# A list scheduler for TensorE's order in a hybrid sequence-mixing layer

## The chip, the cores and the metric

One core of a Trainium2 chip runs the whole layer. The metric is the device time of one execution in microseconds; lower is better. 1493.49 us is the median of three runs of the kernel before.

## What is computed

The input is x, 1024 frames of 1024 channels in float32; 16 learned frames are put in front (L = 1040). Each frame is RMS-normalised, and one projection (`w_in`, 1024 x 7832) gives the inputs of three groups of heads, which run side by side on it. Their outputs, 2048 channels together, go through one output projection (`w_out`), are RMS-normalised and added to the input.

```
hn = rms_norm(h, norm_pre[l])
proj = jnp.einsum("bld,dp->blp", hn, w_in[l])
p_a, p_b, p_c = jnp.split(proj, _splits([P_A, P_B, P_C]), axis=-1)
mixed = jnp.concatenate([
    gated_deltanet_group(p_a, dn_conv[l], dn_A_log[l], dn_dt_bias[l], dn_norm[l]),
    rwkv7_group(p_b, rw_mu[l], rw_w0[l], rw_w2[l], rw_a0[l], rw_a2[l],
                rw_k_k[l], rw_k_a[l], rw_r_k[l], rw_ln_w[l], rw_ln_b[l]),
    mamba2_group(p_c, mb_conv[l], mb_conv_b[l], mb_dt_bias[l], mb_A_log[l], mb_D[l], mb_norm[l]),
], axis=-1)
out = jnp.einsum("blm,md->bld", mixed, w_out[l])
h = h + rms_norm(out, norm_post[l])
```

Group a has 6 heads of 128, group b 8 of 64, group c 12 of 64. Group a is a gated delta rule: in every chunk of frames a triangular system is solved, and a 128 x 128 state is carried from chunk to chunk. Group b is a recurrence with a state per head, done in chunks of 64 frames with a triangular solve as well. Group c is a chunked state-space scan without a solve.

## The kernel before, in words

**Units.** The work after the setup is cut into twelve units: a0 to a5 (one head of group a each), b0 to b3 (two heads of group b), c0 and c1 (six heads of group c), and a thirteenth, o, the output projection. Each unit is a Python generator (`unit_a`, `unit_b`, `unit_c`, `unit_o`) that issues instructions and yields where it would have to wait.

**Projections.** The projection is cut into 61 tiles of 128 output channels. `proj` (line 156) does a tile in pieces of frames, three each (FULL or REAL, 340 to 348 frames, and others for group b), in a PSUM bank `pj`. Float32 accuracy comes from three products in the fast float32r format for each of 8 slices of the inner dimension: rounded weights by rounded input (`hh`), rounded weights by the input's residue (`hl`), the weights' residue by `hh`; 24 products a piece, 72 a tile, in the order slice by slice. `weights` (line 142) loads a tile's weights in two halves: a load on SP, two copies on ScalarE (ACT), and an accumulating load on POOL's queue that leaves the residue. After a tile's first piece, `prefetch` asks for the next tile's weights. Behind each piece an evacuation (`conv`, `shifted` or a gate) takes it out of PSUM on ACT and VectorE (DVE).

**Scans.** A unit first needs some tiles ("proj"), then runs its scan with small float32 products, which TensorE does in two passes each: products of 32x32 and 64x64 that finish the triangular solve (`am`, `bm`), products of 64x128 (`bgr`), transposes (`akT`, `cxT`, ...), and a recurrence over the chunks in which a product, an evacuation on ACT or DVE and the next product follow each other (`aks`, `av`, `ads` in a; `bsi`, `bu`, `bd` in b; `cds`, `cof`, `cdg` in c). `solve32` does the inner 32 x 32 triangular solves on DVE, two small instructions (`s_tmp`, `alb` or `blb`) for each of 30 columns, after a round trip of the blocks through DRAM on SP. In the middle of its scan a unit asks for more tiles with `later` (values, queries, gates), with a due time, and waits for them with `wait`.

**What orders the work.** `schedule` (line 1171) steps the generators by an estimated clock: `Meter` adds up what TensorE's instructions take and a rough lag of the others, and a scan whose lag is over goes ahead of the projection ("fill"), one product of which is issued at a time. `safe` admits a unit only if the 26 tiles of the `s` pool suffice for it. Up to two lanes with two PSUM banks each serve the scans; a third scanning unit shares a lane. So the kernel gives each instruction a place in the program and a priority (`PRI`, `EVA`, `CALM`); which instruction an engine really takes next is then chosen by the framework, which simulates the program with its own estimates and takes, on each engine, the ready instruction with the best priority. That holds for all engines, TensorE's included.

**End.** `unit_o` (line 1080) computes the first half of the output's columns from the mixes that are finished (`po<-ow,ome`), holds until all scans have ended, then does the second half with all sixteen mixes and the rest of the first (`po<-ow,omw`), and writes the output.

## Time and profile before

| | |
|---|---|
| median of 3 runs | 1493.49 us (1492.66 to 1499.25) |
| profiled execution | 1497.37 us, span 1495.2 us |
| TensorE (PE), matmuls | 1439.9 us in flight, 96% of the span, 9657 instructions |
| VectorE (DVE) | 954.8 us, 64% |
| ScalarE (ACT) | 707.2 us, 47% |
| mean granted TensorE clock | 0.956 |
| projection products (pj) | 4392 |
| output products (po) | 768 |

How to read it: the span runs from the first to the last instruction of the profiled execution; the time is a little longer by what lies around it. A matmul in flight is not a matmul at its peak: they are pipelined, and what one costs in a stream is the distance from its start to the next start. PEld is the load of the weights into the array, which runs beside matmuls. The clock is the share of full speed that the chip granted.

### The profile page before, as it was taken

How to read it: one execution, taken by the hardware profiler on the slowest of the kernel's cores; microseconds unless marked ns; L12 is line 12 of the kernel's file. 1: busy time of each engine (PE TensorE's matmuls, PEld its weight loads, DVE VectorE, ACT ScalarE, POOL GpSimd, SP SyncE). 2: the span in 40 equal slices, each digit the busy share in tenths (PEclk: the TensorE clock that was granted, in tenths of full speed). 3: DMA queues.
4: the chain of work that ended last, by engine and by line, in shares of the span. 5: the costliest groups of instructions: out<-in, count | busy, mean ns of one | idle time of the engine just before them, and what ended most of it. 6: DMA issues, size and time to landing. Idle time of an engine off the chain costs nothing.

```text
span 1495.2 us, 26098 instructions
## 1 busy us (share of the span) xinstructions
PE 1439.9 (96%) x9657; PEld 1274.6 (85%) x9657; DVE 954.8 (64%) x2688; ACT 707.2 (47%) x1936; POOL 173.4 (12%) x227
## 2 busy tenths in 40 slices
PE   5999999999999999999999999999999999999897
PEld 4999888888888789989888899889999988678686
DVE  6549485376768347869735787546588867542573
ACT  6455361345444364344746543544577255532530
POOL 2111000000001011111101111001132100200100
PEclk9999898799999799999979999889999999899999
DMA  7344332123223222434322244114534322553851
GB/s 225 87 114 85 81 61 58 43 62 93 51 46 75 67 71 72 116 65 103 76 86 57 62 85 96 29 43 99 118 97 105 71 58 59 171 162 89 259 191 57
DMA packets 120449, 136.28 MB, mean 91 GB/s; under 512 B 39867, under 2 KB 72379, under 8 KB 120323
## 3 DMA queue, kind: packets, MB, share of 16 engines
q1 hardware_dynamic: 102755, 102.64, 23.2%
q0 software_dynamic: 17568, 31.99, 12.7%
q8 instruction: 76, 1.25, 0.3%
q14 instruction: 50, 0.41, 0.1%
HBM read 116.99 MB, written 17.60 MB: 90 GB/s over the span
## 4 chain that ended last, share of the span: by engine, by line
PE 76%; issue 6%; DVE 6%; ACT 6%; DMA 5%; POOL 1%; SPq 0%; DVEq 0%; ACTq 0%; POOLq 0%
PE pj L96 41%; PE po L96 6%; PE bsi L96 5%; PE am L96 3%; PE bgr L96 2%; PE bu L96 2%; PE bm L96 1%; PE aops L96 1%; PE cdg L96 1%; PE ads L96 1%; PE bd L96 1%; PE av L96 1%; PE aks L96 1%; ACT buv L96 1%; DVE s_tmp L96 1%
## 5 line engine op out<-in xcount | busy, mean ns | idle before, releaser
L96 PE MATMUL pj<-hh,w 128*128 128x350 f32 (+8 forms) x2928 | 780.4, 340 | 4.5 <-DMA w<-in_wt_dram 2.7
L96 PEld LDWEIGHTS pj<-hh,w 128*128 128x128 f32 x2928 | 520.4, 193 | 19.4 <-DMA w<-in_wt_dram 2.9
L96 PE MATMUL pj<-hl,w 128*128 128x350 f32 (+8 forms) x1464 | 495.8, 339 | 0.0
L96 PEld LDWEIGHTS pj<-hl,w 128*128 128x128 f32 x1464 | 283.3, 193 | 6.1 <-issue 0.9
L152 POOL DMA_DIRECT2D w<-in_wt_dram x122 | 106.1, 870 | 903.5 <-ACT w L150 676.1
L150 ACT ACTIVATE w<-wr 128x512 fp32r<-128x512 f32 x122 | 76.6, 628 | 62.4 <-PE pj L96 61.2
L96 PE MATMUL po<-ow,omw 128*128 128x512 f32 x408 | 95.7, 395 | 4.1 <-ACT omw L1066 3.7
L96 PEld LDWEIGHTS po<-ow,omw 128*128 128x128 f32 x408 | 77.2, 191 | 22.6 <-ACT omw L1066 5.2
L96 PE MATMUL po<-ow,ome 128*128 128x512 f32 x360 | 92.0, 404 | 2.6 <-ACT ome L1066 1.2
L96 PEld LDWEIGHTS po<-ow,ome 128*128 128x128 f32 x360 | 67.8, 192 | 18.1 <-POOL ow L1049 2.1
L151 ACT CAST w<-wr 128x512 fp32r<-128x512 f32 x122 | 74.3, 609 | 0.1
L96 DVE TENSOR_TENSOR buv<-bu,b_ib 64x128 f32<-64x128 f32 x68 | 19.1, 281 | 81.2 <-PE bu L96 81.2
L96 PE MATMUL bsi<-buv,bgm 64*64 64x64 f32 (+1 forms) x528 | 62.1, 240 | 0.0
L96 DVE TENSOR_TENSOR alb<-alb,s_tmp 33x30 f32<-33x30 f32 (+9 forms) x180 | 56.7, 315 | 3.2 <-POOL alb L96 2.1
L96 DVE TENSOR_TENSOR s_tmp<-alb 33x30 f32<-33x30 f32 (+9 forms) x180 | 57.7, 320 | 1.1
L96 PEld LDWEIGHTS bsi<-buv,bgm 64*64 64x64 f32 (+1 forms) x528 | 42.6, 140 | 17.7 <-issue 3.2
L96 DVE SCALAR_TENSOR_TENSOR b_s<-bd,b_wc,b_s 64x64 f32<-64x64 f32 x120 | 33.9, 282 | 27.2 <-PE bd L96 23.1
L830 ACT COPY by<-bsi 64x128 f32<-64x128 f32 x64 | 16.8, 262 | 70.1 <-PE bsi L96 69.3
L96 ACT COPY b_x<-bsi 64x128 f32<-64x128 f32 x68 | 17.5, 258 | 62.7 <-PE bsi L96 62.4
L183 DVE SCALAR_TENSOR_TENSOR cbc<-pj,pack,cbc 128x346 f32<-128x346 f32 (+4 forms) x72 | 40.3, 567 | 9.8 <-ACT cbc L180 9.2
L1067 DVE TENSOR_TENSOR ome<-omre,ome 128x512 fp32r<-128x512 f32 (+2 forms) x40 | 22.9, 605 | 34.1 <-ACT ome L1066 34.0
L96 PE MATMUL bgr<-bar,bbk 64*128 64x128 f32 x272 | 42.4, 328 | 0.4 <-DVE bgm L96 0.4
(325 smaller groups left out, 2456.5 us busy)
## 6 DMA issues: line engine op xcount, KB each, us to landing
wr<-in_wt_dram SPq DMA_DIRECT2D x122, 256.0 KB, 3.4
w<-in_wt_dram POOLq DMA_DIRECT2D x122, 256.0 KB, 4.9
or<-in_w_out_dram SPq DMA_DIRECT2D x32, 256.0 KB, 4.2
omrw<-d_mix SPq DMA_DIRECT2D x32, 256.0 KB, 4.6
clt<-d_cs SPq DMA_DIRECT2D x24, 256.0 KB, 4.9
omre<-d_mix SPq DMA_DIRECT2D x24, 256.0 KB, 2.6
btw<-d_tw SPq DMA_DIRECT2D x8, 544.0 KB
x<-in_x_dram SPq DMA_DIRECT2D x8, 512.0 KB, 7.5
```

What stands on the lines that cost most here:

```text
L96: return op(out, *args, **kw)
L150: nc.scalar.activation(w[:, 1], raw, AF.Copy, scale=-1.0)
L151: nc.scalar.copy(w[:, 0], raw)
L152: nc.gpsimd.dma_start(w[:, 1], src, accum_op=ADD)
L183: nc.vector.scalar_tensor_tensor(acc[:, a + z: b], p[:, o + z - s: o + b - a - s], cw[:, 3 - s: 4 - s], acc[:, a + z: b], MUL, ADD)
L830: nc.scalar.copy(yt[hs[(c - 1) % 2], (c - 1) // 2, :], pq[64:128, 0:128])
L1067: nc.vector.tensor_tensor(t[:, 1], raw, t[:, 0].bitcast(F32), SUB)
```

## The change

`Meter` and its clock are gone. Each engine is wrapped by a `Scribe`: inside the scheduled part an instruction isn't issued but noted (`write`) in its unit's queue for that engine, with what it depends on (`Access`, `Pool`: which tiles and buffers it reads and writes), an estimated duration and a class (scan, pj, ev, ld, calm, off). A loop in `schedule` then takes, over all engines, the instruction that can start first by these estimates and issues it (`emit`). For TensorE it keeps rounds: after at least BURST (1.0 us) of projections it lets scan products in, and stays with them as long as another is ready within JOIN (0.25 us), first those that write the tile of the one before; where no projection is ready, a scan product goes at once; and where a decaying measure of the array's recent work (`heat`, each product weighted by the share of the array that it fills) is below COLD, it takes a projection. For the other engines it takes the first ready, with a small handicap by class (LESS).

Each TensorE instruction is tied to the one before it by an order-only dependency. Instructions of the other engines get none; they go to the framework in the order in which the loop issues them, and the framework chooses among the ready ones. The priorities PRI, EVA and CALM are no longer set.

A unit's scan starts only on a lane that no other unit holds. A unit's tiles count as given back when its noted instructions have been issued. The gates of a and c are projected in two pieces of 512 frames (HALF) instead of three. `proj` runs the 16 products with the rounded weights first and then the 8 with their residue, and asks for the next weights ahead of the fourth product of the first piece. The units' order (PLAN) differs; a4 and a5 ask for their gate early (SOON); one output weight instead of three is loaded ahead (NOA). At the end of `unit_o` the first half's Square and product stand behind the second half's products, and the closing steps of each row block form a task of their own.

The diff, cut to its core (in `write` only the estimates of TensorE and VectorE are shown; the units' yields lose their lag arguments):

```diff
+HALF = ((16, 528), (528, 1040))
...
-LOOK, LATE, EVAC, DMA = 0.05, 0.3, 2.0, 5.0
-NOA = 3
-PIPE = 0.5
+NOA = 1
 HURRY, DUES = 60, (50, 60, 45, 55, 25, 60)
 GATE = 9
-XP = 500
 XG = ((0, 1), (2, 3), (4, 5, 6), (7, 8))
-PRI, EVA, CALM = 300, 700, 1500
+BURST, JOIN = 1.0, 0.25
+COOL, COLD = 3.0, 0.36
+LESS = {"scan": 0.0, "ev": 0.3, "ld": 0.5, "calm": 1.0, "off": 0.4}
+AHEAD = 8
 NOW = 16
-PLAN = "a0 b0 b1 b2 c0 b3 a1 a2 a3 c1 a4 a5"
+PLAN = "a0 b0 b1 a1 c0 b2 a2 c1 b3 a3 a4 a5"
 GB = (2, 2)
 NT = 3
-SLOW = 1.0
...
+SOON = (4, 5)
 PEAK = {"a": 7, "b": 12, "c": 14, "o": 24}
 LB = PADB + L
...
+        i = Instr()
+        i.go, i.eng, i.cls, i.task, i.done, i.start = (lambda: op(out, *args, **kw)), key, self.cls, self.task, None, None
+        is_ap = lambda x: hasattr(x, "ap") and hasattr(x, "tensor")
...
+        if key == "PE":
+            rows, cols = args[0].shape[0], int(np.prod(args[0].shape[1:]))
+            fast = name == "matmul" and args[0].dtype == F32R
+            i.mode = (r(rows), r(cols), fast)
+            i.step = (n / 2400 + 0.013 if fast else 0.109 if name == "transpose" else
+                      0.063 if r(cols) == 32 else 2 * max(0.058 if r(cols) == 64 else 0.112, n * 0.00085))
+            i.work = rows * cols / 16384 * n * (1 if fast or name == "transpose" else 2) / 2400
+            i.extra = {128: 0.165, 64: 0.108, 32: 0.07}[r(cols)]
...
+        elif key == "DVE":
...
+            i.step = 0.065 + n * (0.00116 if len(ins) > 2 else 0.00105)
+            i.extra = 0.085
+            i.lock = sum("PSUM" not in str(x.space) and x.size() > x.shape[0] for x in ins) > 1
...
+    def emit(self, i, start):
+        r = i.go()
+        ins, was = r.ins, self.before.get(i.eng)
+        if i.eng != "PE":
+            pass
+        elif was is None:
+            self.tc.keep_in_program_order(r)
+        else:
+            self.tc.add_manual_dep(ins, was, mybir.DependencyInfo(mybir.DependencyClass.NoSync, mybir.DependencyReason.DATA), reason="order")
+        self.before[i.eng] = ins.name
+        if i.eng == "PE":
+            if self.array and self.array != i.mode:
+                if self.array[:2] != i.mode[:2]:
+                    start += 0.093
+                if i.mode[2] and not self.array[2]:
+                    i.step += 0.1
+            self.array = i.mode
+        self.free[i.eng] = start + i.step
...
+            steps = [(kt, 0, h) for kt in range(KT) for h in (self.hh, self.hl)] + [(kt, 1, self.hh) for kt in range(KT)]
...
+                with self.of(cls="pj"):
                     self.engines[2].matmul(p[:, : b - a0], w[kt // 4][:, x, kt % 4, :], h[:, kt, a0:b],
-                                           start=(kt == 0 and m == 0), stop=(kt == KT - 1 and m == 2))
-                    yield
-            with self.tc.high_priority(EVA):
+                                           start=(j == 0), stop=(j == len(steps) - 1))
+                yield
+            with self.of(cls="ev"):
                 evac(p, a, b, a - a0)
-            if n == 0:
-                self.prefetch(i)
...
+    def gate_a(self, h, z):
...
+        return self.later(18 + h, self.proj(18 + h, HALF, gate), DUES[2])
...
         asked = self.later(h, self.conv(h, self.ctap_a[:, h, :], q, pieces=REAL), DUES[1])
+        z = None
+        if h in SOON:
+            yield 8
+            z = self.one([128, SEQ], f"az{h}")
+            gated = self.gate_a(h, z)
...
+            gates.append(self.later(41 + 3 * u + j, self.proj(41 + 3 * u + j, HALF, lambda p, a, b, o: nc.scalar.copy(
...
     def o_product(self, p, mx, ws, start=True, stop=True):
         for i, (k, w) in enumerate(ws):
             for j, (l, r) in enumerate(((0, 0), (0, 1), (1, 0))):
-                self.engines[2].matmul(p, mx[k][l], w[:, r, :], start=(start and i == 0 and j == 0),
-                                       stop=(stop and i == len(ws) - 1 and j == 2))
+                with self.of(cls="pj"):
+                    self.engines[2].matmul(p, mx[k][l], w[:, r, :], start=(start and i == 0 and j == 0),
+                                           stop=(stop and i == len(ws) - 1 and j == 2))
             yield
...
             halves, s1, s2 = [ob[m][:, 512 * n: 512 * n + 512] for n in range(2)], ss[:, m, 0:1], ss[:, m, 1:2]
+            def second():
+                v.tensor_tensor(halves[1], p, npost[:, 512:], MUL)
+                act.activation(p, p, AF.Square, accum_out=s2)
+            if m < 2:
+                second()
+            p0 = None
             if late:
                 p0 = bank(m)
                 yield from self.o_product(p0, mx, wl)
                 v.tensor_tensor(halves[0], halves[0], p0, ADD)
-            act.activation(halves[1], halves[0], AF.Square, accum_out=s1)
-            v.tensor_scalar(s1, s1, D * EPS, None, ADD)
-            v.tensor_tensor(halves[0], halves[0], npost[:, 0:512], MUL)
             if m > 1:
                 p = bank(m)
                 yield from self.o_product(p, mx, w)
-            v.tensor_tensor(halves[1], p, npost[:, 512:], MUL)
-            act.activation(p, p, AF.Square, accum_out=s2)
-            rs = self.sm.tile([128, 1], F32, tag="ors", name="ors", bufs=2)
-            v.tensor_tensor(s1, s1, s2, ADD)
-            self.rsqrt(rs, s1, "or")
-            for n in range(2):
-                cols = slice(512 * n, 512 * n + 512)
-                v.scalar_tensor_tensor(halves[n], halves[n], rs, xr[:, cols], MUL, ADD)
-                nc.sync.dma_start(a["out"][rows, cols], halves[n])
+                second()
+            act.activation(p if p0 is None else p0, halves[0], AF.Square, accum_out=s1)
+            v.tensor_tensor(halves[0], halves[0], npost[:, 0:512], MUL)
+            with self.of(self.tail(), "ev"):
+                rs = self.sm.tile([128, 1], F32, tag="ors", name="ors", bufs=2)
+                v.tensor_scalar(s1, s1, D * EPS, None, ADD)
+                v.tensor_tensor(s1, s1, s2, ADD)
+                self.rsqrt(rs, s1, "or")
+                for n in range(2):
+                    cols = slice(512 * n, 512 * n + 512)
+                    v.scalar_tensor_tensor(halves[n], halves[n], rs, xr[:, cols], MUL, ADD)
+                    nc.sync.dma_start(a["out"][rows, cols], halves[n])
...
+        self.queue.append({"tile": i, "gen": gen, "due": self.free["PE"] + due, "done": False})
...
-            if ready and (when(ready[0]) <= self.clock + LOOK or not can):
-                s = ready[0]
-                self.clock = max(self.clock, when(s))
-                if s["lane"] is None:
-                    used = [sum(o["lane"] == g for o in active) for g in range(len(GB))]
-                    s["lane"] = used.index(min(used))
-                self.lane = s["lane"]
-                with self.tc.high_priority(CALM if s["calm"] else PRI):
+        round_, since, last, heat, self.seen_at = False, BURST, None, 1.0, 0.0
...
+                for s in list(active):
+                    if s["kind"] != "scan" or s["drop"] and s["want"] is None or s["task"].q["PE"] or s["task"].n > AHEAD:
+                        continue
+                    if s["on"] and not s["on"]["done"] or not safe(s):
+                        continue
+                    if s["lane"] is None:
+                        open_ = [g for g in range(len(GB)) if all(o["lane"] != g for o in active)]
+                        if not open_:
+                            continue
+                        s["lane"] = open_[0]
+                    self.lane = s["lane"]
                     step(s)
...
+                        more = True
+        while True:
+            advance()
+            best = None
+            for e in ENGINES:
+                heads = []
+                for t in self.tasks:
+                    if t.q[e]:
+                        i = t.q[e][0]
+                        r = self.ready(i)
+                        if r is not None:
+                            heads.append((self.begins(i, r), r, i))
+                if not heads:
+                    continue
+                if e == "PE":
+                    now = self.free["PE"]
+                    pj = min((h for h in heads if h[2].cls == "pj"), key=lambda h: h[0], default=None)
+                    sc = [h for h in heads if h[2].cls != "pj"]
+                    sc = min(sc, key=lambda h: (h[0] > now + 0.02 if h[2].out == last else 1, h[0]), default=None)
+                    if pj is None or sc is None:
+                        pick = sc or pj
+                    elif heat * float(np.exp((self.seen_at - now) / COOL)) < COLD:
+                        pick = pj
+                    elif round_:
+                        pick = sc if sc[0] <= max(now + JOIN, pj[0]) else pj
+                    else:
+                        pick = sc if since >= BURST and sc[0] <= max(now + 0.03, pj[0]) or sc[0] < pj[0] - 0.3 else pj
+                else:
+                    first = min(h[0] for h in heads)
+                    pick = min((h for h in heads if h[0] <= first + 0.05), key=lambda h: h[1] + LESS[h[2].cls])
+                if best is None or pick[0] < best[0]:
+                    best = pick
...
+            if i.eng == "PE":
+                was = self.free["PE"]
+                if i.cls == "pj":
+                    since = since + i.step if not round_ else i.step
+                    round_ = False
+                else:
+                    round_ = True
+                last = i.out
+                heat = heat * float(np.exp((self.seen_at - start) / COOL)) + i.work / COOL
+                self.seen_at = start
+            self.emit(i, start)
+            self.tasks = [t for t in self.tasks if t.n or t is self.loader or t is self.mixer or any(t is s["task"] for s in active) or fill and (
+                t is fill.get("task") or fill.get("unit") and t is fill["unit"]["task"]) or planned and planned.get("unit") and t is planned["unit"]["task"]]
```

## Rows read from the trace of the kernel before

**Rows 1.** The page, its head and slices; the clock by core.

```profile
PE 1439.9 (96%) x9657; PEld 1274.6 (85%) x9657; DVE 954.8 (64%) x2688; ACT 707.2 (47%) x1936; POOL 173.4 (12%) x227
...
PE   5999999999999999999999999999999999999897
...
PEclk9999898799999799999979999889999999899999
...
core 0: 1495.2 us, clock 0.956
```

**Rows 2.** Waits of TensorE, longest total first: total us, times, longest.

```profile
PE xT L260 <- DVE x L255: 10.9, 1, 10.9
PE xT L260 <- DVE hl L264: 7.3, 5, 2.6
PE po L96 <- ACT omw L1066: 3.7, 1, 3.7
PE bm L96 <- DVE bdd L779: 2.8, 1, 2.8
PE pj L96 <- DMA w<-in_wt_dram: 2.7, 1, 2.7
```

**Rows 3.** Windows at the low clock; below, two windows of the projections (pj) alone.

```profile
core 0: us, PE busy (x) PEld busy (x) DVE busy (x) ACT busy (x) POOL busy (x), PEclk, DMA share, GB/s
...
248.10:282.30 34.20, 34.20 (x174) 25.87 (x175) 10.01 (x22) 6.08 (x17) 0.88 (x1) 0.50 0.07 12
...
sum 131.10, PE 125.61 PEld 102.38 DVE 37.82 ACT 35.79 POOL 5.59; mean PE 11.42 PEld 9.31 DVE 3.44 ACT 3.25 POOL 0.51
...
248.10:282.30 34.20, 5.20 (x13) 3.43 (x14) 0.00 (x0) 0.00 (x0) 0.50 0.07 12
282.30:316.40 34.10, 24.45 (x119) 18.28 (x119) 7.98 (x15) 4.60 (x9) 1.00 0.30 68
```

**Rows 4.** Timeline of TensorE, two scans at once: start us, us, what.

```profile
246.00 0.48 PE L96 MATMUL bgr<-bar,bbk 64*128 64x128 f32 x2
246.41 0.24 PE L96 MATMUL bm<-bdd,bgm 32*32 32x32 f32 x2
246.58 0.49 PE L96 MATMUL bgr<-bar,bbk 64*128 64x128 f32 x4
...
250.38 0.79 PE L96 MATMUL bgr<-bar,bbk 64*128 64x128 f32 x2
251.10 0.31 PE L96 MATMUL bm<-bdd,bgm 32*32 32x32 f32 x2
251.34 0.79 PE L96 MATMUL bgr<-bar,bbk 64*128 64x128 f32 x2
```

**Rows 5.** Timeline around a 32x32 excursion; around a 128x128 excursion.

```profile
239.97 0.52 PE L96 MATMUL pj<-hh,w 128*128 128x386 f32 x2
240.32 0.33 PE L96 MATMUL pj<-hl,w 128*128 128x386 f32 x1
...
241.03 0.33 PE L96 MATMUL pj<-hh,w 128*128 128x386 f32 x1
241.29 0.69 PE L96 MATMUL bm<-bdd,bgm 32*32 32x32 f32 x16
241.91 0.44 PE L96 MATMUL pj<-hh,w 128*128 128x386 f32 x1
242.19 0.34 PE L96 MATMUL pj<-hl,w 128*128 128x386 f32 x1
...
604.26 0.33 PE L96 MATMUL pj<-hl,w 128*128 128x386 f32 x1
604.43 0.81 PE L96 MATMUL cds<-ctmp,cbt 128*128 128x192 f32 x4
604.95 0.65 PE L96 MATMUL pj<-hh,w 128*128 128x386 f32 x2
605.43 0.34 PE L96 MATMUL pj<-hl,w 128*128 128x386 f32 x1
```

**Rows 6.** The first and the last change from projections to scan work.

```profile
52.06 0.32 PE L285 MATMUL pjs<-hl,ws_hl 128*64 128x346 f32 x1
52.30 1.44 PE L290 MATMUL p<-pack,p 64*16 64x24 f32 x12
...
1316.72 3.33 PE L96 MATMUL po<-ow,ome 128*128 128x512 f32 x14
1321.58 0.66 PE L96 MATMUL aoT<-pack,avt 128*128 128x128 f32 x4 [1.52 <-DVE avt L96]
```

**Rows 7.** Output products of 512 columns: 14 from 1483.83, the last 6 from 1485.64.

```profile
1483.83 3.33 PE L96 MATMUL po<-ow,omw 128*128 128x512 f32 x14
...
1485.64 1.52 PE L96 MATMUL po<-ow,omw 128*128 128x512 f32 x6
```

**Rows 8.** Waits of ScalarE and of SP's queue at the weights.

```profile
ACT w L150 <- PE pj L96: 61.2, 39, 8.9
...
SPq L149 <- ACT w L151: 578.1, 88, 28.0
```

**Rows 9.** The window where the output begins; the output weights' loads (page, issues).

```profile
1295.00:1332.00 37.00, 32.24 (x159) 24.33 (x158) 23.32 (x53) 18.86 (x51) 6.48 (x5) 1.00 0.61 193
...
or<-in_w_out_dram SPq DMA_DIRECT2D x32, 256.0 KB, 4.2
```

**Rows 10.** Timeline near the end: Square of a first half, a product on VectorE.

```profile
1477.04 0.63 ACT L1144 ACTIVATE ob<-ob 128x512 f32<-128x512 f32 x1
...
1487.20 0.69 DVE L1150 TENSOR_TENSOR ob<-po,npost 128x512 f32<-128x512 f32 x1 [5.97 <-PE po L96]
```

**Rows 11.** The solve's steps on VectorE (page, costliest groups).

```profile
L96 DVE TENSOR_TENSOR s_tmp<-alb 33x30 f32<-33x30 f32 (+9 forms) x180 | 57.7, 320 | 1.1
```

**Rows 12.** First transposes and last ones of the scans: first and last start us.

```profile
L96 PE MATMUL akT<-pack,ak x54: 270/272/331, 76.4 to 1130.3; 128*128 128x128 f32 x48, 128*16 128x128 f32 x6
...
L96 PE MATMUL aoT<-pack,avt x48: 270/273/330, 227.7 to 1322.4; 128*128 128x128 f32 x48
```

More of the change, by code (lines that the diff above doesn't have):

```diff
@@ L76, in nt, with __init__ @@
     return NM if c == 0 else 128
-class Meter:
-    def __init__(self, trunk, engine, fixed, each):
-        self.trunk, self.engine, self.fixed, self.each = trunk, engine, fixed, each
+class Instr:
+    __slots__ = ("go", "eng", "deps", "cls", "step", "extra", "mode", "work", "lock", "took", "start", "done", "task", "out")
+class Task:
+    def __init__(self, name):
+        self.name, self.q = name, {e: [] for e in ENGINES}
+        self.n = 0
+ENGINES = ("PE", "ACT", "DVE", "POOL", "SP")
+SEES = {"PE": 0.055, "ACT": 0.035, "DVE": 0.035, "POOL": 0.075, "SP": 0.027}
@@ L110, in off, with of @@
-    @contextmanager
-    def off(self):
-        self.aside = True
-        yield
-        self.aside = False
+        self.nc = nc = Engines(self, tc.nc)
+        self.engines = (nc.vector, nc.scalar, nc.tensor, nc.gpsimd, nc.sync)
+        self.seen, self.born, self.task, self.cls = {}, {}, None, "scan"
+        self.before, self.free = {}, {e: 0.0 for e in ENGINES}
+        self.array, self.bus, self.held = None, 0.0, {"DVE": 0.0, "POOL": 0.0}
+    @contextmanager
+    def of(self, task=None, cls=None):
+        was = self.task, self.cls
+        self.task, self.cls = task or was[0], cls or was[1]
+        yield
+        self.task, self.cls = was
@@ new lines, in ready, with begins @@
+    def ready(self, i):
+        if i.start is None:
+            t = 0.0
+            for d in i.deps:
+                if d.done is None:
+                    return None
+                if not d.eng == i.eng == "PE":
+                    t = max(t, d.done + SEES[i.eng])
+            i.start = t
+        return i.start
+    def begins(self, i, t):
+        t = max(t, self.free[i.eng])
+        if i.lock:
+            other = self.held["POOL" if i.eng == "DVE" else "DVE"]
+            if t < other:
+                t = other + 0.02
+        return t
@@ L142, in weights, with halves @@
     def weights(self, i):
+        if self.writing:
+            with self.of(self.loader, "ld"):
+                return self.halves(i)
+        return self.halves(i)
+    def halves(self, i):
         nc = self.nc
@@ L1052, in o_mixed, with o_mixed_ @@
     def o_mixed(self, m, ks, name, ahead=False):
+        if self.mixer not in self.tasks:
+            self.tasks.append(self.mixer)
+        with self.of(self.mixer, "ld"):
+            return self.o_mixed_(m, ks, name, ahead)
+    def o_mixed_(self, m, ks, name, ahead):
         nc, out = self.nc, {}
@@ L1224, in choose @@
             soon = min(self.queue, key=lambda q: q["due"], default=None)
[L1225 removed]
+            if soon and soon["due"] < self.free["PE"] + HURRY:
                 self.queue.remove(soon)
```

350 lines of the change are left out of this document (241 added, 109 removed).

## The prediction

> **What bounds the kernel now.** First the page: TensorE has work in flight for 96% of the span, VectorE for 64%, and no slice between the first and the last is below 8 tenths [rows 1]. So the other engines cover their work, and the question is what TensorE does with its time. Next its waits: apart from the setup's transposes (10.9 and 7.3 us) no line waits over 4 us in total [rows 2]. TensorE hardly ever waits, and still it is not at its best. Three views show why.
>
> The windows show the clock. The mean granted clock is 0.956 [rows 1], that is (1 - 0.956) x 1495.2 / 0.5 = 131 us at the lower of the two levels, 1.2 instead of 2.4 GHz; eleven stretches, of which [rows 3] holds the longest and the sum, 131.1 us. In the longest, 34.2 us, TensorE was never idle, but only 13 projection matmuls ran; in the equally long stretch behind it, at full clock, 119 did [rows 3]. Before the clock fell the engine had alternated small scan products [rows 4].
>
> The timeline shows the changes of kind. Projections of 386 columns start every 0.175 us. Around 16 products of 32x32 the last start before comes 0.26 us ahead of them, and the first projection after takes 0.28 us: 0.19 us lost, and another change lies between, on leaving the small shape. Around four passes of 128x128 nothing is lost on entry, and the next two projections take 0.48 instead of 0.35 us [rows 5]. I went through all starts from 45 us on: projections give way to scan work 564 times; [rows 6] holds the first and the last. Away from the low clock, an excursion costs 0.27 us over the pitch of its own instructions (520 of them, waits included), an adjacent pair with different array shapes 0.09 us (633 pairs), and 349 of the 564 projection runs are shorter than 1.0 us, 211 us together.
>
> Third, where two scans have products ready at once, the framework alternates them one by one: two 64x128 passes, two 32x32 passes, 0.58 us a turn at full clock, 0.96 us at half [rows 4].
>
> **The change, part by part.** The profiled execution took 1497.4 us (span 1495.2, 2.2 around it), 3.9 over the median of 1493.5. The sum is made against it.
>
> *Clock.* The new choice takes a projection whenever the recent array work, weighted by shape, falls below COLD. The 126.5 us of low clock in which TensorE worked held what 63 us would do at full clock. Bounds: 0 gained (no projection has its weights or its tile slots at that time) to 63. I take two thirds, **-42**: most stretches follow the small products of the triangular solves, with projections in between, which can be denser.
>
> *Rounds.* A round of scans opens after at least 1.0 us of projections, unless no projection is ready. The 211 us of short runs then make at most 211 runs in place of 349, so 138 excursions go; with bursts of 2 us 240 would. I take 170. One that is merged into a neighbour keeps its own shape change and saves the way back: 0.13 us by the 128x128 row, up to 0.31 us by the 32x32 row with the change inside; 0.2 us is between, so **-34**. Bounds 0 (everything saved is waited for instead) and 240 x 0.31 = -74. The Trainium skill, TensorEngine Tiling (Array Packing), Key Properties, says that changing the tiling mode, not just the tile, drains the engine. By that alone only the excursions with another shape than 128x128 count, 257 of the 520, and the saving would be 170 x 0.49 x 0.2 = 17 us, by this estimate 17 us less; the trace agrees on the shape changes, but also shows the 0.13 us of a return at equal shape, so I keep the sum by rows.
>
> *Same tile first.* Within a round the scheduler stays on one output bank. 322 changes between scan shapes at 0.09 us are 29 us; a third away, **-10** (bounds 0 and -20).
>
> *Gates in two pieces.* Twelve tiles lose 24 of 72 matmuls, 288 in all, the columns unchanged. 8 products of 512 columns take 1.81 us, 0.226 each, against 0.213 of columns at 2.4 GHz [rows 7]: 0.013 us fixed, **-4**.
>
> *Weights.* The projection first runs the 16 products with w and then the 8 with the residue, and asks for the next weights after 3 products, not 24. For each tile two SP loads, four ACT copies and two POOL loads move forward by 21 products, 3.7 us at 0.175. On SP and POOL they pass later loads and stores of the scans. ACT now stands up to 8.9 us at the first of the copies, behind which its evacuations queue; SP stands longer still behind the copies, off the path [rows 8]. TensorE waited for weights once, 2.7 us [rows 2]. Taken as 0; if ACT's stand goes, ACT is what is free earlier, and nothing waits on that now. With the cover gone those 2.7 us come back.
>
> *Order of units, two lanes, earlier gates for a4 and a5, one output weight ahead instead of three.* A unit starts its scan only on a free lane; now a third shares one. Two output weights load later; in the stretch where the output begins TensorE is busy 32.24 of 37 us [rows 9], and two loads of 4.2 us [rows 9] come on top: between 0 and +8.4, I take **+3**. The output's Square and product of the first half are written behind the last product, 0.63 + 0.69 us [rows 10]; their input is there 48 products or 10.9 us earlier, so 0, or +1.3 if they are queued late.
>
> *Waits.* TensorE's order is now fixed from estimated durations, while VectorE, ScalarE, POOL and SP run in the order that the framework finds with its own. Each scan product that comes late holds every product behind it, projections too. Inside a round the plan also accepts 0.25 us. With 394 excursions left: nothing for most, 0.25 us at one in four, is **+24**; bounds -20 (TensorE's present waits in the scans go) and 394 x 0.32 = +126, one solve step of VectorE [rows 11] ahead of the awaited evacuation in every round. I stand near the low end, since the framework's choice for those engines leaves TensorE few waits now [rows 2].
>
> Sum: -42 - 34 - 10 - 4 + 3 + 24 = -63, so 1434 in a profiled execution and 1430 beside the median.
>
> **Rivals.**
> *Two lanes too few (slower).* Twelve scans, each from its first akT, bw or cxT to its last aoT, byT or cyT, last 152, 180, 181, 185, 157, 199 (a), 265, 290, 240, 290 (b), 272 and 248 us (c), 2659 together, from 76.4 to 1322.4 us [rows 12]; three overlap at times. Two lanes need 1330, so the last ends at 1406; behind it come 408 products with all mixes, 93 us, and 8 of the tail: span 1507, 1505 beside the median. For it: bursts of 1 us stretch each step of a recurrence, and units wait while slots drain. Against: present scans stand behind small changes and the third sharer, and an eighth off each brings the end to 1240. It sets the end if the scans shorten by less than 6%, and makes it slower than before under 1%; idle lanes raise both. Chance 0.08.
> *Late evacuations (slower).* If VectorE's or ScalarE's order puts one 0.32 us step ahead in every round, the waits are +126 instead of +24: 1532. At 0.22 us a round the gain is gone. For it: ACT already stands in front of products that the framework thought nearer, 8.9 us at worst [rows 8]. Against: TensorE waits little behind them now [rows 2]. With milder forms between, 1500 to 1532, chance 0.09; forms that end at no change have 0.06.
> *Only half of it.* The clock stays at 0.956 because no projection fits when the small products come, as in the 34 us with 13 of them: 1430 + 42 = 1472. Or the order does not do what it says, the scans being ready too rarely together for rounds, 564 excursions as before: 1430 + 34 = 1464. Chance 0.18.
> *All of it.* Clock full, 240 excursions less, no added waits: 1493.5 - 63 - 74 - 20 - 4 = 1332 at the end; between there and the forecast, about 1385. Chance 0.15.
> My forecast, 1400 to 1460, has 0.44.
>
> **Numbers.** A measurement of this kernel tells about 0.5%, 7.5 us, from no change. Faster: 0.44 + 0.18 + 0.15 = 0.77; same 0.06; slower 0.08 + 0.09 = 0.17. The range 1375 to 1508 takes in the forecast, the halves, the lanes and half of the best case, and leaves out the other half (0.07) and the upper late evacuations (0.08). The likeliest side alone would be 1375 to 1475.
>
> **What would show it.** Right: mean clock 0.98 or more, no half-clock stretch over 15 us; under 430 excursions, few runs under 1 us; 9369 TensorE instructions; waits of TensorE behind VectorE and ScalarE of 20 to 60 us in all. Wrong: a clock still near 0.956 (first term); many waits of a pj or scan row on ACT or DVE, over 100 us (waits); an output that begins after 1300 us with TensorE idle before it and the last aoT after 1350 (lanes). The forecast as a whole falls if the time is over 1486.

## The result, and the profile after

The changed kernel takes 1514.05 us (median of four, 1506.95 to 1518.49) beside 1496.12 for the kernel before (also of four): ratio 1.0122, interval 1.0078 to 1.0166. It is slower, by 1.2%. The forecast was 1430; the time lies 6 us above the range, which ended at 1508, and on the other side of the kernel before. The profiled execution took 1513.7. Medians here hold every execution, while ratios leave out those marked slow, over 1.5% above the fastest of their kernel.

The page of the changed kernel: span, busy time, slices of TensorE and of its clock; then the clock by core.

```profile
span 1511.8 us, 25439 instructions
...
PE 1421.2 (94%) x9369; PEld 1248.2 (83%) x9369; DVE 965.6 (64%) x2674; ACT 701.3 (46%) x1916; POOL 173.4 (11%) x227
...
PE   5999999998999889989999999989899999899897
...
PEclk9999899999999999999997999999699989799999
...
core 0: 1511.8 us, clock 0.956
```

Against [rows 1]: 288 TensorE instructions fewer and 19 us less busy time, but eight slices at 8 where there was one, and the clock where it was. Next the windows at the low clock (columns as in [rows 3]): the two longest, one of the next, and the sum of all fourteen.

```profile
core 0: us, PE busy (x) PEld busy (x) DVE busy (x) ACT busy (x) POOL busy (x), PEclk, DMA share, GB/s
...
176.91:190.56 13.65, 13.65 (x68) 11.46 (x67) 5.31 (x19) 5.94 (x14) 1.73 (x2) 0.50 0.38 78
...
811.79:828.85 17.06, 17.06 (x82) 14.99 (x81) 4.54 (x9) 6.00 (x13) 1.73 (x2) 0.50 0.17 34
...
1057.55:1081.44 23.89, 19.82 (x92) 14.54 (x91) 7.11 (x33) 7.64 (x34) 0.00 (x0) 0.50 0.12 38
...
sum 133.41, PE 115.56 PEld 95.81 DVE 63.33 ACT 47.37 POOL 9.42; mean PE 8.25 PEld 6.84 DVE 4.52 ACT 3.38 POOL 0.67
```

The total is that of before, 133.4 against 131.1 us, in fourteen stretches instead of eleven. TensorE now also idles in them: 17.9 us, against 5.5. Then its waits behind the setup, longest total first, beside [rows 2] (total us, times, longest):

```profile
PE po L210 <- ACT ome L210: 6.6, 1, 6.6
PE bbon L210 <- ACT buv L210: 6.4, 4, 3.9
...
PE czT L210 <- DVE ctmp L210: 5.0, 1, 5.0
PE po L210 <- ACT po L210: 4.6, 1, 4.6
PE agk L210 <- DVE alo L210: 3.7, 7, 0.8
PE bd L210 <- DVE buv L210: 3.6, 9, 0.8
PE cdg L210 <- issue: 3.1, 1, 3.1
```

Behind the setup no line waited over 3.7 us in total before; now there are longer ones, and many small ones of every kind of scan. The five longest single waits behind it (3.9, 3.1, 5.0, 6.6 and 4.6 us, in order of time) end at 369.6, 529.4, 1011.5, 1290.1 and 1427.4 us. Each reaches into a stretch at the low clock:

```profile
368.05:374.88 6.83, 5.29 (x28) 3.88 (x28) 3.92 (x8) 2.07 (x6) 0.16 (x1) 0.50 0.25 45
528.48:535.31 6.83, 5.96 (x23) 5.99 (x24) 4.86 (x18) 4.61 (x16) 0.00 (x0) 0.50 0.02 7
...
1009.76:1016.59 6.83, 5.12 (x19) 5.12 (x20) 5.35 (x17) 2.10 (x9) 0.00 (x0) 0.50 0.20 43
...
1286.24:1293.07 6.83, 2.96 (x10) 2.49 (x11) 4.51 (x9) 5.18 (x15) 1.50 (x2) 0.50 0.99 303
...
1426.18:1433.01 6.83, 5.60 (x13) 4.44 (x14) 6.16 (x15) 4.46 (x12) 0.00 (x0) 0.50 0.41 123
```

Together they are 34 of the 133.4 us. The kernel before had one such pair, its wait of 3.7 us just ahead of a stretch of 3.4. So the like totals hide a change of kind: 99 us in the other stretches against 128 before.

To see where the span went I took, for every TensorE instruction, the time to the next start less the pitch of its own shape at full clock (its **excess**). The pitches sum to 1237.5 us before and 1233.8 after; the 3.7 are the gates. The excess:

| us | before | changed |
|---|---|---|
| at the low clock | 69.8 | 67.1 |
| projection after projection | 63.4 | 56.9 |
| into a scan and back | 40.3 | 34.7 |
| scan product after scan product | 50.2 | 86.3 |
| before 45 us (setup) | 14.6 | 13.7 |
| sum | 238.3 | 258.7 |

Excursions from projections to scan work fell from 564 to 405, projection runs under 1 us from 349 to 4. Starts over 0.2 us late at full clock (**late starts**, below) rose from 41.6 to 76.5 us, and the longest stretch of scan work without a projection from 13 to 34 us. That stretch shows what went wrong. Windows from 1040 us on, first of all work, then of the projections (pj) alone:

```profile
1040.00:1050.00 10.00, 9.90 (x153) 8.36 (x152) 7.29 (x27) 9.01 (x32) 0.00 (x0) 1.00 0.01 2
...
1050.00:1084.00 34.00, 27.65 (x149) 20.30 (x147) 12.34 (x48) 14.98 (x56) 3.83 (x4) 0.65 0.26 78
...
1084.00:1094.00 10.00, 9.62 (x63) 7.95 (x64) 2.93 (x11) 2.19 (x7) 0.15 (x1) 1.00 0.14 28
...
1040.00:1050.00 10.00, 5.08 (x26) 3.77 (x25) 2.25 (x4) 0.99 (x2) 1.00 0.01 2
...
1050.00:1084.00 34.00, 0.21 (x2) 0.08 (x1) 2.23 (x4) 1.00 (x2) 0.65 0.26 78
```

Apart from some transposes and opening products of a3 (`akT`, `agk`) and c1's last transposes, b3's recurrence alone holds TensorE, many of its steps waiting for another engine, and the clock falls. TensorE's timeline in it (start, length, idle before):

```profile
1055.70 0.46 PE L210 MATMUL bsi<-b_s,bar 128*128 128x128 f32 x2 [0.39 <-ACT by L210]
1056.09 0.44 PE L210 MATMUL bsi<-buv,bgm 64*64 64x64 f32 x4
1057.35 0.55 PE L210 MATMUL bu<-b_x,bgm 64*64 64x64 f32 x4 [0.83 <-ACT b_x L210]
1058.28 0.80 PE L210 MATMUL bd<-buv,bbt 128*128 128x128 f32 x2 [0.37 <-DVE buv L210]
```

The scheduler's own timetable (its planned starts, matched to TensorE's order one by one) has this hole, 23.9 us long: the next tile is the value projection of a3, which unit_a asks for only after its agk products. The same match gives the size of the whole miss: the last output product was planned 1338.9 us behind the first scheduled one and came 120.6 us later. About 59 of these arose inside the stretches at the low clock, 75 if the waits that reach into them are counted whole.

### The profile page after: what moved, and what is told of

The parts are those of the page before. It is cut to its first block, busy times and chain, and to the rows that moved or that the text cites. A ratio compares the mean times of both kernels' runs of the same rounds, so it can differ in the third digit from the quotient of the medians.

```text
span 1511.8 us, 25439 instructions
## 1 busy us (share of the span) xinstructions
PE 1421.2 (94%) x9369; PEld 1248.2 (83%) x9369; DVE 965.6 (64%) x2674; ACT 701.3 (46%) x1916; POOL 173.4 (11%) x227
## 4 chain that ended last, share of the span: by engine, by line
PE 70%; DVE 14%; ACT 6%; DMA 5%; issue 3%; POOL 0%; SPq 0%; DVEq 0%; ACTq 0%; POOLq 0%
PE pj L210 34%; PE po L210 9%; PE bsi L210 4%; DVE s_tmp L210 2%; PE am L210 2%; PE bgr L210 2%; PE bu L210 2%; PE cdg L210 1%; DMA or<-in_w_out_dram 1%; DVE blb L210 1%; PE bm L210 1%; PE bd L210 1%; ACT w L210 1%; PE aops L210 1%; DMA x<-in_x_dram 1%
## 5 line engine op out<-in xcount | busy, mean ns | idle before, releaser
L210 PE MATMUL pj<-hh,w 128*128 128x350 f32 (+7 forms) x2688 | 729.7, 347 | 0.0
L210 PEld LDWEIGHTS pj<-hh,w 128*128 128x128 f32 x2688 | 482.1, 193 | 24.7 <-issue 2.4
L210 PE MATMUL pj<-hl,w 128*128 128x350 f32 (+7 forms) x1344 | 463.9, 348 | 0.0
L210 PEld LDWEIGHTS pj<-hl,w 128*128 128x128 f32 x1344 | 259.9, 193 | 12.7 <-issue 1.1
L210 ACT ACTIVATE w<-wr 128x512 fp32r<-128x512 f32 x120 | 75.3, 627 | 80.0 <-PE pj L210 74.2
L210 PE MATMUL po<-ow,omw 128*128 128x512 f32 x432 | 101.0, 396 | 4.6 <-ACT po L210 4.6
L210 PEld LDWEIGHTS po<-ow,omw 128*128 128x128 f32 x432 | 82.9, 192 | 22.5 <-ACT po L210 5.0
L210 PE MATMUL po<-ow,ome 128*128 128x512 f32 x336 | 87.4, 410 | 6.6 <-ACT ome L210 6.6
L210 PEld LDWEIGHTS po<-ow,ome 128*128 128x128 f32 x336 | 62.9, 194 | 19.5 <-ACT ome L210 7.1
L210 PEld LDWEIGHTS bsi<-buv,bgm 64*64 64x64 f32 (+1 forms) x528 | 43.1, 142 | 17.9 <-issue 3.8
L210 DVE TENSOR_TENSOR s_tmp<-blb 68x30 f32<-68x30 f32 (+14 forms) x120 | 39.5, 329 | 23.8 <-DMA blb<-d_l 21.3
L210 DVE SCALAR_TENSOR_TENSOR b_s<-bd,b_wc,b_s 64x64 f32<-64x64 f32 x120 | 33.9, 282 | 26.7 <-PE bd L210 25.1
L210 DVE SCALAR_TENSOR_TENSOR a_s<-a_s,sc_etot,ads 128x128 f32<-128x128 f32 x42 | 14.4, 344 | 44.6 <-PE ads L210 44.4
```

The costliest lines, as they stand in the source:

```text
L210: i.go, i.eng, i.cls, i.task, i.done, i.start = (lambda: op(out, *args, **kw)), key, self.cls, self.task, None, None
```

## Experiments

Three theories stood first. **A**: the other engines leave the plan, so TensorE meets products that it planned ready; tying them all to the plan helps. **B**: the plan itself, its two lanes and its estimates, is no better than the old order. **C**: an order fixed from estimates makes TensorE stand at every product that comes later than estimated; less tie or more allowance helps. Ratios are to the kernel before, run beside each.

**Which engines are tied.** The edit is the one line in emit, `if i.eng != "PE": pass`: no engine skipped, all skipped, PE, DVE and ACT tied, PE alone free.

```
-        if i.eng != "PE":
+        if i.eng == "":                           (all five tied)
+        if i.eng:                                 (none tied)
+        if i.eng not in ("PE", "DVE", "ACT"):     (three tied)
+        if i.eng == "PE":                         (all but TensorE tied)
```

All: 

> All five engines are tied to the list scheduler's order, nothing else differs from the changed kernel (1514 us). Theory A (the framework's order on VectorE, ScalarE and the queues departs from the one that TensorE's order was planned with, and so TensorE waits): about 1450 us or less, TensorE's starts late by over 0.2 us sum to well under the 76 us of the changed kernel, about 45. Theory B (the plan itself, its rounds and two lanes, is not better, its estimates are off): 1500 us or more, the late starts stay over 70 us.

None: 

> No engine is tied: the framework gets the instructions in the scheduler's order and chooses on all engines, TensorE too. Theory A: TensorE's order then fits that of the others again, about 1480 us, with more excursions than the 415 of the changed kernel but fewer late starts. Theory B: no better than the changed kernel, 1505 to 1530 us, since units, lanes, rounds and gates are the same.

Three: 

> TensorE, VectorE and ScalarE tied, POOL and SP free. Theory A with the evacuations as the cause: as with all engines tied, within 10 us of it. If it is the loads' order on SP and POOL that matters, it stays near 1514 us.

All but TensorE: 

> The reverse of the change: VectorE, ScalarE, POOL and SP tied to the scheduler's order, TensorE free. Theory C with TensorE's tie as the main cause: 1480 to 1505 us, since tying all engines after TensorE cost 30 us more and TensorE can now step round a late product. If any tie costs by itself, 1515 us or more.

Measured: all 1544.1, 1.037 (1.030 to 1.043); none **1472.0, 0.990 (0.983 to 0.996)**; three 1551.9, 1.044 (1.036 to 1.052); all but TensorE 1546.3, 1.028 (1.022 to 1.034). Tying more engines beside TensorE costs more, and tying all but TensorE costs too, where C had 1480 to 1505. So the remedy of A falls; that the other engines leave the plan is not refuted, for none tied came out as A had it (about 1480, fewer late starts). With no tie the very same planner is 2.2% better than the changed kernel: what loses is holding TensorE to the plan. None tied also beats the kernel before by 1.0%, but the gates in two pieces alone give 0.6% (below), so this run does not decide on B; what speaks against B is the untied kernel with the longer allowance, 3.7% better (below). None tied has 567 excursions, as many as before, 45.6 us of late starts and no stretch without a projection over 7.7 us.

**The rules of the planner.** Rounds off (BURST and JOIN 0) with TensorE tied and with none tied; the clock's rule off (COLD 0); the rule "same tile first" off; the units in the old order. TensorE is tied in all but the second.

```
-BURST, JOIN = 1.0, 0.25
+BURST, JOIN = 0.0, 0.0
...
-COOL, COLD = 3.0, 0.36
+COOL, COLD = 3.0, 0.0
...
-sc = min(sc, key=lambda h: (h[0] > now + 0.02 if h[2].out == last else 1, h[0]), default=None)
+sc = min(sc, key=lambda h: h[0], default=None)
...
-PLAN = "a0 b0 b1 a1 c0 b2 a2 c1 b3 a3 a4 a5"
+PLAN = "a0 b0 b1 b2 c0 b3 a1 a2 a3 c1 a4 a5"
```

Rounds off, tied: 

> BURST and JOIN are 0, so scans go ahead as soon as they are ready; TensorE alone is tied. If rounds cost more by the waits inside them than they save in changes of kind: faster than 1514 us by 10 to 30, with over 550 excursions. If they save what was forecast (0.2 us for each excursion): slower by 20 to 35 us. Theory A makes no difference here: late starts stay at 70 us or more.

Rounds off, none tied: 

> No engine tied, and BURST and JOIN 0: the framework chooses everywhere, from an order without rounds. Against the untied kernel with rounds (1472 us): if rounds serve only to give a fixed order its slack, no difference, within 10 us. If they are what improves the order, 1500 us or more and over 620 excursions.

Clock's rule off: 

> TensorE tied; COLD is 0, so the rule that takes a projection after weak array work never applies. If the rule keeps the clock up: mean clock under 0.956 and slower than 1514 us by 10 to 30. If it hardly finds a projection to take, or its measure is not the chip's: clock 0.95 to 0.96 and within 8 us of 1514.

Same tile first off: 

> TensorE tied, without the rule that a product into the same tile goes first. My forecast had 10 us for that rule: if it holds, mode changes between scan products rise and the time is 5 to 15 us above the changed kernel's 1514, 1515 to 1530. Rival (the rule makes long trains of one unit wait on themselves): fewer late starts and 1495 to 1510.

Old order of units: 

> TensorE tied, but the units in the order of the kernel before (a0 b0 b1 b2 c0 b3 a1 a2 a3 c1 a4 a5). If the units' order made the stretch of 34 us without a projection at 1050 and so the loss, that stretch goes and the time falls to 1475 to 1495. If a tied order loses on any plan because products come later than planned, 1500 to 1530 with late starts above 65 us and another stretch of over 15 us somewhere.

Measured: rounds off 1725.9 (1.158, 1.151 to 1.166; 830 excursions) tied and 1537.7 (1.021, 1.014 to 1.028; 690) free, so within this planner rounds are needed. Tied, the loss is far over the 20 to 35 us that I expected; the low clock's excess alone goes from 67 to some 210 us. Clock's rule off 1519.8 (1.011, 1.005 to 1.017) and same tile first off 1510.4 (1.008, 1.004 to 1.012): neither differs from the changed kernel's 1.012; the two rules give nothing that can be measured. Old order of units 1527.3 (1.017, 1.009 to 1.024): the hole of 34 us goes and three others open, of 33, 28 and 26 us; the longest is shown here in its windows, all work and then projections in the middle of it:

```profile
397.90:430.90 33.00, 24.61 (x120) 17.67 (x121) 8.86 (x28) 7.95 (x27) 0.88 (x1) 0.57 0.15 32
...
404.00:411.00 7.00, 0.00 (x0) 0.00 (x0) 0.00 (x0) 0.00 (x0) 0.50 0.00 0
```

**The allowance.** SEES["PE"] is what the planner adds after an operand is done before TensorE can use it: 0.055 us, then 0.355 and 0.655.

```
-SEES = {"PE": 0.055, "ACT": 0.035, ...
+SEES = {"PE": 0.355, "ACT": 0.035, ...
```

0.355, TensorE tied: 

> TensorE alone tied, as in the changed kernel, but the plan counts every result of another engine as visible to TensorE 0.3 us later (SEES 0.355 instead of 0.055), so that scan products stand later in TensorE's order. Theory C (a fixed order makes TensorE stand at every product whose input is later than estimated): late starts over 0.2 us fall from 76 to about 40 us, the time to 1470 to 1490 us. Theory B (two lanes and rounds stretch the scans): each step is 0.3 us longer, the last aoT later than 1370 us and the time over 1514 us.

0.655, TensorE tied: 

> TensorE tied, the planner's allowance for a product's operands 0.655 us in place of 0.055 (0.355 gave 1480). Theory C: late starts fall on, to 55 to 65 us, and the time stays at 1465 to 1485. Rival (the allowance only lucks into another order with fewer stretches at the half clock): the time jumps without a trend, anywhere from 1470 to 1515, and follows the low clock's excess (32 us there, 67 us in the changed kernel), not the late starts.

0.355, none tied: 

> No tie on any engine and the allowance of 0.355 us. If both gains add, 1450 to 1465. If the framework, once free, makes the same of any emission order, the same as without the allowance, 1468 to 1480 and some 570 excursions.

0.655, none tied: 

> No tie and the allowance at 0.655 us. If a longer allowance as such leaves less waiting, 1425 to 1440. If 0.355 fits what operands really take and more only puts products off, 1440 to 1460. If the gain of the 0.355 run was the luck of one order, anything from 1435 to 1480 with the low clock's excess deciding.

**Where the projections stand.** Only the scans' products tied; that with 0.355 us; and, to see whether the hole is the cause, TensorE tied but for one tile's or twelve tiles' projections.

```
-        if i.eng != "PE":
+        if i.eng != "PE" or i.cls == "pj":                   (scans alone tied)
+        if i.eng != "PE" or i.out.startswith("pj15_"):       (tile 15 free)
...
-        self.before[i.eng] = ins.name
+        if i.cls != "pj":                            (scans alone tied; for freed tiles, theirs in its place)
+            self.before[i.eng] = ins.name
```

Scans alone tied: 

> Only the scans' products are tied to the planner's order; the projections and output products (class pj) go wherever the framework puts them. If the fixed order costs because a product that comes late holds the projections that stand behind it (theory C), projections are again free to fill the stretch of 34 us without any at 1050, and the time falls to what no tie gave, 1465 to 1485, with no scan run over 15 us. If the fixed order of the products among themselves costs (a late product of one unit holds ready products of the other lane), the time stays at 1500 to 1520 and late starts stay above 70 us.

Scans alone tied, 0.355: 

> Only the scans' products tied, as in the run that gave 1467, and the planner's allowance at 0.355 us. If tied projections are one loss and the short allowance another, both gains add here as they did with no tie: 1430 to 1450, late starts 30 to 40 us. If the allowance helps only where the framework may also move products, 1460 to 1475.

Tile 15 free: 

> TensorE tied but for the 72 projections of one tile (15, the value projection of a3), which stand first behind the stretch of 34 us; the planner's own timetable has that stretch too, 24 us of it, since it asks for this tile only after the products of a3's agk. If tied projections cost because they can't move into such stretches, they run inside it, the stretch is cut to under 15 us and the time falls by the 12 to 20 us that it lost: 1495 to 1502. If the loss is spread over all of TensorE's order, 1508 or more even with that stretch filled.

Twelve tiles free: 

> The same with the value and query tiles of all six a units free (tiles 0 to 5 and 12 to 17, of some 57), everything else tied. If what the tie costs is that tiles asked late can't be drawn forward, 1480 to 1495, most of the way to the 1467 with every projection free. If each projection's place matters alike, a fifth of the 47 us, 1500 to 1508.

Medians and ratios of these two series, the changed kernel among them:

| allowance us | TensorE tied | scans alone tied | none tied |
|---|---|---|---|
| 0.055 | 1514.1; 1.012 (1.008-1.017) | 1467.0; 0.984 (0.979-0.989) | 1472.0; 0.990 (0.983-0.996) |
| 0.355 | 1480.1; 0.986 (0.980-0.993) | 1449.4; 0.967 (0.960-0.973) | **1435.1; 0.963 (0.958-0.968)** |
| 0.655 | 1492.7; 1.001 (0.998-1.004) | not run | 1460.7; 0.972 (0.964-0.979) |

The columns say what the tie costs: freeing the projections alone gives 47 us back at 0.055 and 31 at 0.355 (42 and 29 by the ratios); freeing the scans' products as well adds nothing that holds in both rows (5 lost, 14 gained). Scans alone tied still left one stretch of 17.8 us without a projection, where I had expected none over 15. None tied at 0.355 beat both cases that I had written down (1450 to 1465, 1468 to 1480). In the trace of "scans alone tied" 1872 of the 4920 projection and output records have fewer scan records ahead of them than in the changed kernel, none has more: **the framework draws projections forward into gaps that the plan leaves**. Against the changed kernel its excess is 45.5 us less, 25.1 of them at the low clock and 27.1 between scan products. The stretch that was a hole, in the kernel with none tied: windows of its projections, and TensorE's timeline.

```profile
1020.00:1030.00 10.00, 5.65 (x25) 3.64 (x24) 2.23 (x4) 1.02 (x2) 1.00 0.71 200
1030.00:1040.00 10.00, 5.07 (x22) 3.10 (x21) 2.23 (x4) 1.00 (x2) 1.00 0.19 65
1040.00:1050.00 10.00, 6.74 (x29) 4.58 (x30) 1.37 (x3) 0.55 (x1) 1.00 0.10 15
...
1027.97 0.42 PE L210 MATMUL pj<-hl,w 128*128 128x348 f32 x1
1028.23 0.80 PE L210 MATMUL pj<-hh,w 128*128 128x348 f32 x4
1028.88 0.38 PE L210 MATMUL bsi<-b_s,bar 128*128 128x128 f32 x2
1029.19 0.44 PE L210 MATMUL bsi<-buv,bgm 64*64 64x64 f32 x4
```

The same products of the same recurrence, with projections where TensorE stood before, at full clock.

The two runs with freed tiles correct the simplest form of this. Tile 15 free measured 1520.7, 1.019 (1.013 to 1.025), twelve tiles free 1514.5, 1.017 (1.010 to 1.023): no gain, though 74 and 493 records moved forward. I had expected 1495 to 1502 for the first if tied projections cost by that hole, 1508 or more if the loss is spread over the order, which is what came; for the second at most 1508, which was missed. Tile 15's windows, all work and then projections:

```profile
1050.00:1078.00 28.00, 27.92 (x208) 23.28 (x208) 15.99 (x55) 19.26 (x65) 4.30 (x5) 1.00 0.33 95
1078.00:1101.00 23.00, 17.36 (x102) 12.82 (x102) 9.71 (x34) 6.36 (x20) 1.43 (x3) 0.70 0.27 57
...
1050.00:1078.00 28.00, 16.91 (x74) 11.44 (x74) 6.72 (x12) 2.99 (x6) 1.00 0.33 95
1078.00:1101.00 23.00, 0.00 (x0) 0.00 (x0) 2.20 (x4) 0.99 (x2) 0.70 0.27 57
```

The hole is filled, and opens again 28 us on, since the tile that filled it is missing where it stood. One hole is not the cause. With every projection free the gain builds up along the span, though not evenly (15 us by 575 us of the changed kernel's time, 33 by 880, between 27 and 48 from 1043 on); that there the next tile follows forward too fits this, but no run separates it.

The rows of the table say that the allowance of 0.355 helps whatever is tied, 18 to 37 us. With TensorE tied, late starts hardly fell (76.5, 68.1 and 71.4 us for the three allowances), against what I expected of C; the low clock's excess did (67.1, 32.3, 48.8, one profiled execution each), and these differences, 35 and 17 us, are near those of the medians, 34 and 13. So the gain of 0.355 over 0.055 is shown, and with TensorE tied it lies in the clock, not in the saved waiting that C foresaw; why the clock gained is not shown. 0.655 being worse again (13 us tied, 26 free; by the ratios 22 and 13, and free the intervals overlap) is not explained either, and part may be the luck of one order.

**The gates alone**, in the kernel before:

```
-            gated = ... self.proj(18 + h, REAL, gate)
+            gated = ... self.proj(18 + h, HALF, gate)
...
-            self.proj(41 + 3 * u + j, REAL,
+            self.proj(41 + 3 * u + j, HALF,
```

> The kernel before with nothing but the gates' projections in two pieces of 512 in place of three (288 matmuls fewer). My sum had 4 us for it: ratio 0.994 to 1.000. Rival: longer pieces hold the scans' products longer and move the clock, 1.000 to 1.010.

Measured 1481.9, 0.994 (0.991 to 0.997), 9 us by the ratio; the pitches lose the 3.7 us counted. The interval, 4.3 to 13 us, begins just above that, and where the rest comes from is open.

**The version that beats both** is none tied with 0.355 us. Its page and clock:

```profile
span 1431.3 us, 25451 instructions
...
PE 1380.6 (96%) x9369; PEld 1218.5 (85%) x9369; DVE 951.7 (66%) x2674; ACT 697.4 (49%) x1916; POOL 174.8 (12%) x227
...
PEclk9999999999999999999999999999997999999999
...
core 0: 1431.3 us, clock 0.983
```

Its excess is 177.8 us, 20.5 of it at the low clock, late starts 32.4, no stretch without a projection over 6.0 us, and 529 excursions: it wins with the clock and the waits, hardly with rounds.

## Why the prediction was wrong

**Clock, -42 forecast: -2.7.** This step failed most. (Its base, 126.5 us of work at the low clock, is 125.6 in [rows 3]; half is 63 either way.) I let the COLD rule take back two thirds of the low clock; its lower bound, no projection with weights and slots at that time, is what came about in the longest stretch (none ran from 1057.6 to 1081.4). The sign that I had named for this, a clock still near 0.956, came. The rule orders only what is there, and its own removal changed nothing. In the second longest, 811.8 to 828.9, TensorE was busy throughout and 36 projections ran, 11.6 us of the 17.1; the clock fell behind a train of 32x32 products (808.3 to 811.1 us). There projections were present and did not bring it back at once. And the term left out that the change makes new waits: the five stretches that long waits reach into hold 34 us, about what the other stretches lost (128 to 99). Whether the waits brought the clock down, no run separates.

**Rounds, -34: -12.** The count held (159 excursions gone, 170 forecast; short runs 4). The value per excursion didn't: those between 128x128 products alone, cheapest to begin with, fell most (263 to 175 at full clock), the costly ones with other shapes from 257 to 206. Entry, return and projection pitch together give 5.6 + 6.5 = 12.1 us, 0.08 each instead of 0.2; without the late starts that these rows hold it is about 16 us, 0.10 each. The Trainium skill, TensorEngine Tiling (Array Packing), Key Properties, says that a change of the tiling mode, not of the tile alone, drains the engine. The trace agrees on the changes themselves: 0.09 us median before and after. The estimate by that rule alone was 17 us, and the measured 12 lies nearer to it than to mine; with the 51 excursions of another shape that really went, at 0.2 us, the estimate would be 10.

**Same tile first, -10: about -3.5 by count** (changes of shape between scan products 322 to 283, at 0.09), nothing by its own run.

**Gates, -4: -3.7** in pitch.

**Waits, +24: +36** between scan products (late starts of all kinds +35). The size is 12 us off, but the mechanism was too narrow as well. I priced a wait at one product in four; the dearer part of a fixed order is that no projection may pass the product that waits, which the scans-alone run prices at 47 us (42 by the ratio), waits and clock together. I had written that a late product holds projections too, and put no number on it.

These terms, -2.7 - 12.1 - 3.7 + 36.1 and -0.9 for the setup, make +16.7; the span grew by 16.6. That they meet is bookkeeping, for every start is counted in one row. **Output weights, +3**, are spread over them: TensorE waited 6.6 us for a mix where the output begins (2.6 in all at these products before), and ScalarE's copy of that mix stood behind three copies of output weights that had waited 2.7 and 0.9 us for their loads. The projection weights moved forward stood as priced: ScalarE waited 74.2 us at its copies, 61.2 before, and no line of TensorE waits for them.

**The rivals.** *Two lanes too few* did not set the end as I had summed it: the scans lasted 2323 us together instead of 2659, an eighth less, as I argued against it, and the output began ahead of the last aoT. But that aoT came at 1363.1, 41 us later than before and past the 1350 that I had named as a sign:

```profile
L210 PE MATMUL po<-ow,ome x336: 387/389/795, 1282.6 to 1397.9; 128*128 128x512 f32 x168
...
L210 PE MATMUL aoT<-pack,avt x48: 272/273/421, 237.9 to 1363.1; 128*128 128x128 f32 x48
```

By the match with the timetable, eight of the ten scans behind the first two began 1 to 10 us after another had given its lane free, so the lanes do hold the scans. What speaks against them as the cause of the loss is that the kernels with rounds and with none or only the scans tied have the same two lanes and are 42 to 79 us faster; a third lane was not tried.

*Late evacuations* has the time in its band, 1500 to 1532, but not by its road: +126 us of waits were to come, +36 came, and holding VectorE and ScalarE to the plan made it worse. It was *only half of it* for the clock, with more waits on top. My chance of 0.17 for slower was too low, as I see it, because three gains, clock, rounds and same tile, all hung on the plan having projections wherever it wanted them.

## What to carry to other kernels

Tie to a hand-made schedule only the instructions whose order is the gain (here even the scans' tie gained nothing that holds); leave the filler free, because a fixed order bars it from the gaps that the plan leaves. A forecast for such a schedule should ask at each term whether the work that it wants to place is there at that time, and price the fall-back at zero. When one gap is filled by drawing work forward, look for the gap that it leaves.

## What the runs showed of the hardware that was not expected

The half clock (1.2 instead of 2.4 GHz) came with TensorE busy all of 811.8 to 828.9 and 176.9 to 190.6 us, projections among its work, so neither idleness nor the lack of projections marks all of these stretches, though five of the fourteen began within a wait of TensorE of 3.1 to 6.6 us. What sets it in each is left open. The decay rows' broadcast loads (clt, 256 KB) landed 8.0 us after issue (median) in the changed kernel against 4.9 before, and 4.5 to 8.0 in the other runs whose view gives it; the planner's formula puts such loads at 4.2 or 5.0.
